# Loads of a unit's r, k, key norms and v placed between the rate products of its preparation (RWKV-7 / sliding-window decoder step)

## The chip, the cores and the metric

The kernel runs on one core of a Trainium2 chip. The core has TensorE (PE; the loading of its weights is shown as PEld), VectorE (DVE), ScalarE (ACT), GpSimd (POOL) and SyncE (SP), which issues nearly all transfers of this kernel (the DMAs). Each engine works through its own instructions in order, and semaphores tie the engines together. The metric is the device time of one execution in microseconds; the median of three runs of the kernel before is 2142.66 us (2141.24 to 2144.08).

## The reference

One inference step of a two-layer trunk for a prompt of 256 tokens, with 16 meta tokens in front, and 8 single-token samples: 280 columns in all. Layer 0 is RWKV-7 time mixing with 64 heads of 64; layer 1 is sliding-window attention with a shared K/V and sinks. The change lies in layer 0. Cut to what matters:

```python
r, k, v, z = (xm[:, :, i] @ w_rkvz[i] for i in range(4))
w_log = -softplus(-(w0 + tanh(xw @ w1) @ w2)) - 0.5
decay = exp(-exp(w_log))
a = sigmoid(a0 + (xa @ a1) @ a2)
kk = k * k_k; kk = kk / max(sqrt(sum(kk * kk, -1)), 1e-12)
k = k * (1 + (a - 1) * k_a); b = kk * a
def rwkv7_step(S, inp):                       # scanned over the tokens
    sa = einsum('bhij,bhj->bhi', S, kk)
    S = S * d - sa[..., None] * b + v[..., None] * k
    return S, einsum('bhij,bhj->bhi', S, r)
y = groupnorm(y) * gn_g + gn_b + sum(r * k * r_k) * v
out = (y * silu(z)) @ w_out
```

Decay and `a` come from two low-rank products, the "rates".

## The kernel before

**Stages.** A first stage normalises the inputs and makes the first k and v products. Then comes phase A, the longest one with several things going on at once; then the output product of layer 0, the shared K/V, layer 1's q and z products with the attention between them, and its output product. All large products run as three fp32r matmuls (high x high, high x low, low x high), whose weights are split into a high and a low part by ScalarE and VectorE (`split`, L183 to L187) as they arrive, five buffers deep.

**Phase A** (`phase_a`, `drive`). `products` lists 64 products of 256 output columns (r, k, v, z, and a first part of the output product), each of 16 *pieces* of six matmuls. `drive` takes one piece after another, and before each it visits generators ("streams"): epilogues of products, `main`, `preps`, `decodes` (the samples), late gates, and side streams such as the group norm. A stream yields a number of pieces to wait, and where needed a condition; it is resumed at the first piece at which both hold. `mark` notes the piece at which something was done, and `after(n, ...)` asks whether it was marked at least n pieces ago. So TensorE's order is written out by hand: what a stream emits on TensorE stands where the piece counter is. The other engines' order is not: the framework's scheduler orders each of them by a simulated timeline in which TensorE's order is fixed, so that a load or a vector operation may stand far ahead of its place in the source, once its inputs and its buffer are free there. One thing holds it back: what a stream other than the first two emits on VectorE is put behind the weight split emitted last but one (`issue_after(self.los[-2].ins)` in `drive`).

**Units.** The 64 heads are 16 units of 4 heads. `preps` prepares unit after unit with `prep(u)`:

- it loads the low-rank weights and visits TensorE four times, 3 to 4 pieces apart, for the rates (`ps_l`, L870 to L872);
- it then waits for the products of r, k, v and, from unit 4 on, for the key norms (`('n', g)`), loads kT, rT and the norms (spread over the rows into kk, L552, two transfers), and forms kk, k, a, the decays' running sum and their exponentials (L887 to L914);
- from unit 4 on it waits for the group norm of the pair two before (`('g', u // 2 - 2)`), since vT of four units ago is then given back after its store to `yd` (L1250), and loads vT (L917);
- it gathers the samples' columns on POOL (L921), turns them on TensorE (`ps_sm`, L924) eight pieces later, and makes two "bonus" products (`ps_bo`, L940), 5 and 4 pieces later. Every visit of TensorE with a `pp_free` condition also waits until a PSUM bank, shared with the epilogues of k and v and the decodes, has had three pieces.

kT has two buffers, rT and kk have one, vT four. `prep_e(u)` forms the matrices KB and E from them (L956 to L968) and is the last reader of rT and kk. For an even unit it runs right behind `prep`; for an odd one `main` runs it (mark `e`), once the pair's chain is done (`u`), the odd unit is prepared (`p`) and the even unit's scores are (`c`). `main` then makes the odd unit's scores (21 pieces), solves the triangular systems (24 + 4 + 7 + 5 = 40), and runs the chain over five chunks of tokens (48); the group norm of the pair ends 46 pieces after its chain (`g`). `preps` begins the next even unit at `e`.

At the end of phase A the gates of the last four blocks are split (`late_gates`, tiles ghi and glo), which the output product `ps_oa` reads first.

Of the kernel before, what the change touches and what calls it, by code (L numbers as in the profile page):

```python
# [109 lines left out]
class Kernel:  # L110
# [736 lines left out]
    def prep(self, u):  # L847
        nc, rp, I = self.nc, self.rp, self.I
        V, A, G = nc.vector, nc.scalar, nc.gpsimd
        tt = V.tensor_tensor  # L850
        MU, AD, SU = ALU.mult, ALU.add, ALU.subtract
        dma = nc.sync.dma_start
        p0 = 2 * u
        b, sl = p0 // 4, slice(p0 % 4, p0 % 4 + 2)
        w = lambda n, bufs=1: rp.tile([128, 2, N], F32, tag=n, bufs=bufs, name=f"{n}{u}")

        raw = rp.tile([LR, 512], F32, tag="lraw", name=f"lraw_{u}")
        dma(raw, I['lw2'][u])
        if u:
            yield 3  # L860
        hi = rp.tile([LR, 512], F32R, tag="lhi", name=f"lhi_{u}")
        lo = rp.tile([LR, 512], F32R, tag="llo", name=f"llo_{u}")
        self.split(hi, lo, raw)
        ws = [(hi[:, 256 * i:256 * i + 256], lo[:, 256 * i:256 * i + 256]) for i in range(2)]
        wa = [w("cl"), w("ta")]
        for i, (hi, lo) in enumerate(ws):
            for j in range(2):
                yield 3 if i or j else 4 if u else 14, self.pp_free
                ps = self.pp_bank(f"ps_l{i}{j}_{u}")
                self.mm3(ps[:, :N], hi[:, j * 128:j * 128 + 128], lo[:, j * 128:j * 128 + 128],  # L870
                         self.lt[i][0], self.lt[i][1], True, True)
                A.activation(wa[i][:, j], ps[:, :N], AF.Tanh, scale=0.5,  # L872
                             bias=self.par2[:, 32 * i + p0 + j:32 * i + p0 + j + 1])
        cl, a = wa
        if u >= 4:
            yield 0, self.after(6, ('n', u // 4), *(('x', m, p0) for m in range(3)))
        else:
            yield 0, self.after(6, ('x', 0, p0))
        kT = w("kT", 2)
        dma(kT, self.kd[b][:, sl])  # L880
        rT = w("rT")
        dma(rT, self.rd[b][:, sl])

        kk = w("kk")
        self.spread(kk, self.kr[u // 4][4 * u % 16:4 * u % 16 + 4])
        for j in range(2):
            V.scalar_tensor_tensor(kk[:, j], kT[:, j], self.pcol(P_KK, p0 + j), kk[:, j], op0=MU, op1=MU)  # L887

        for j in range(2):
            km = rp.tile([128, N], F32, tag="sq", bufs=2, name=f"km{j}_{u}")  # L890
            A.activation(km, a[:, j], AF.Identity, scale=self.par2[:, 64 + p0 + j:65 + p0 + j],
                         bias=self.par2[:, 96 + p0 + j:97 + p0 + j])
            tt(kT[:, j], kT[:, j], km, op=MU)
        A.activation(a, a, AF.Identity, scale=-0.5, bias=self.half[:, 1:2])
        tt(a, a, kk, op=MU)
        A.activation(cl, cl, AF.Identity, scale=0.5, bias=self.half[:, 0:1])

        for j in range(2):
            V.tensor_tensor_scan(cl[:, j, :L], self.reset, cl[:, j, :L], 0.0, op0=MU, op1=AD)

        Pp = self.Pp
        ch = lambda x: x[:, :, :256].rearrange("p q (c t) -> p q c t", t=64)
        pch = Pp[:, :, :260].rearrange("p q (c t) -> p q c t", t=65)
        for j in range(2):
            A.activation(pch[:, j, :, 1:65], ch(cl)[:, j], AF.Exp, scale=-CD)
        A.activation(Pp[:, :, 261:N + 5], cl[:, :, 256:N], AF.Exp, scale=-CD)
        A.activation(cl, cl, AF.Exp, scale=CD)
        if u % 2 == 0:
            self.PC = rp.tile([128, 4, 5], F32, tag="PC", bufs=2, name=f"PC{u}")
        PC = self.PC[:, 2 * (u % 2):2 * (u % 2) + 2]  # L910
        A.copy(PC[:, :, 0:4], pch[:, :, :, 64])
        A.copy(PC[:, :, 4:5], Pp[:, :, 276:277])

        if u >= 4:  # L914
            yield 0, self.after(0, ('g', u // 2 - 2))
        vT = w("vT", 4)
        dma(vT, self.vd[b][:, sl])  # L917

        sm = rp.tile([128, 2, 6, NS], F32, tag="sm", name=f"sm{u}")
        for i, x in enumerate((kk, a, kT, rT, vT, Pp[:, :, 5:])):  # L920
            G.tensor_copy(sm[:, :, i], x[:, :, L:N])  # L921
        yield 8, self.pp_free
        ps = self.pp_bank(f"ps_sm{u}")
        nc.tensor.transpose(ps[:96, :128], sm.rearrange("p a b c -> p (a b c)"), self.ident)  # L924
        sr = rp.tile([96, 2, 64], F32, tag="sr", name=f"sr{u}")
        A.copy(sr, ps[:96, :128].rearrange("p (h j) -> p h j", h=2))
        g, h0 = p0 // 8, (2 * p0) % 16
        for j in range(2):
            dma(self.vecd[g][:, :, h0 + 2 * j:h0 + 2 * j + 2].rearrange("v b h j -> (v b) (h j)"),
                sr[48 * j:48 * j + 48].rearrange("p h j -> p (h j)"))  # L930

        def rk_of(j):
            rk = rp.tile([128, L], F32, tag="sq", bufs=2, name=f"rk{j}_{u}")
            V.scalar_tensor_tensor(rk, rT[:, j, :L], self.pcol(P_RK, p0 + j), kT[:, j, :L], op0=MU, op1=MU)
            return rk
        rk = [rk_of(j) for j in range(2)]
        for j in range(2):
            yield 5 - j if u > 1 else 3, self.pp_free
            ps = self.pp_bank(f"ps_bo{j}_{u}")
            nc.tensor.matmul(ps[:, :L], self.cr[C_BO], rk[j], start=True, stop=True)  # L940
            tt(vT[:, j, :L], ps[:, :L], vT[:, j, :L], op=MU)
            A.activation(vT[:, j, :L], vT[:, j, :L], AF.Identity, bias=self.pcol(P_GB, p0 + j))
        self.U[u] = dict(PC=self.PC, bonus=vT, kT=kT, rT=rT, kk=kk, a=a, cl=cl)
# [998 lines left out]
```

## Time and profile before

| | |
|---|---|
| median of 3 runs | 2142.66 us (2141.24 to 2144.08) |
| profiled execution | 2148.06 us, span 2146.2 us |
| granted TensorE clock over the span | 0.992 |
| weights and other transfers | 446.29 MB, 208 GB/s, DMA engines 66.6% busy on the main queue |
| phase A, 142 to 1306 us | TensorE 1133.8 of 1164.0 us busy, VectorE 905.3, ScalarE 750.6, POOL 98.4 |

The page gives busy times of each engine, the span in slices, the chain of work that ended last, and groups of instructions. Names such as `ps_bo<-rk` are tiles of the program, written and read; `L940` is a line of the kernel. In a list of waits, `PE ps_sm L924 <- POOL sm L921: 2.3, 2, 2.0` means that TensorE stood idle before line 924 until POOL's line 921 was done, 2.3 us in total, twice, 2.0 us at the longest. `SPq` is SP's issuing queue: its time is the issue of a transfer, not the transfer.

### The profile page before, as it was taken

To read this page: it belongs to the slowest core of one execution; us is meant where nothing else is said; L and a number is where in the kernel's file an instruction comes from. 1 tells how busy PE (TensorE), PEld (TensorE's weight loads), DVE (VectorE), ACT (ScalarE), POOL (GpSimd) and SP (SyncE) were. 2 spreads that over 40 slices of the span, in tenths; PEclk is the share of its full clock that TensorE was granted. 3 is DMA by queue.
4 is the path that set the end of the run, shared out by engine and by line. 5 is a ranking of instruction groups with operands and counts; after the bars stand their busy time and mean duration, and the time that the engine had idled before them with its cause. 6 is when DMAs were issued, how large, how long until landed. Compare 5 with 4: busy or idle time off the path is not lost.

```text
span 2146.2 us, 56094 instructions
## 1 busy us (share of the span) xinstructions
PE 2098.6 (98%) x21548; PEld 1993.0 (93%) x21548; DVE 1705.8 (79%) x4080; ACT 1260.3 (59%) x2757; POOL 137.0 (6%) x196
## 2 busy tenths in 40 slices
PE   9999999999999999999999999999999999999997
PEld 7999998899898988898989999999999999999997
DVE  7966767787687777888988787987888888878885
ACT  3456756576765666767666444565565565544443
POOL 0011100011010010100200000100000000000000
PEclk9999999999999999999999999999999999999999
DMA  7998667658756766676656777867445454677774
GB/s 256 311 322 244 194 204 226 205 176 280 221 169 188 240 227 191 212 220 201 208 160 201 232 228 242 239 191 231 146 136 171 145 153 133 172 216 240 224 229 134
DMA packets 275589, 446.29 MB, mean 208 GB/s; under 512 B 53288, under 2 KB 97000, under 8 KB 274928
## 3 DMA queue, kind: packets, MB, share of 16 engines
q1 hardware_dynamic: 274888, 441.66, 66.6%
q8 instruction: 169, 2.77, 0.5%
q10 hardware_dynamic: 432, 1.05, 0.1%
q14 instruction: 100, 0.82, 0.1%
HBM read 381.69 MB, written 65.03 MB: 208 GB/s over the span
## 4 chain that ended last, share of the span: by engine, by line
PE 85%; DVE 5%; DMA 4%; ACT 3%; issue 2%; SPq 0%; POOL 0%; DVEq 0%; POOLq 0%; ACTq 0%
PE ps_z L208 6%; PE ps_z L209 6%; PE ps_z L210 6%; PE ps_r L208 3%; PE ps_ob L208 3%; PE ps_ob L210 3%; PE ps_v L208 3%; PE ps_ob L209 3%; PE ps_q L208 3%; PE ps_q L210 3%; PE ps_q L209 3%; PE ps_k L208 3%; PE ps_r L209 3%; PE ps_r L210 3%; PE ps_v L209 3%; PE ps_v L210 3%
## 5 line engine op out<-in xcount | busy, mean ns | idle before, releaser
L208 PE MATMUL ps_z<-mhlm,whi_z 128*128 128x280 f32 x512 | 158.6, 310 | 0.7 <-ACT st L779 0.7
L208 PE MATMUL ps_q<-bmh,whi_qb 128*128 128x264 f32 x512 | 150.0, 293 | 0.1
L209 PE MATMUL ps_z<-mhlm,whi_z 128*128 128x280 f32 x512 | 149.9, 293 | 0.0
L210 PE MATMUL ps_z<-mhlm,wlo_z 128*128 128x280 f32 x512 | 149.5, 292 | 0.0
L208 PE MATMUL ps_z<-bmh,whi_zb 128*128 128x264 f32 x512 | 147.5, 288 | 0.0
L210 PE MATMUL ps_q<-bmh,wlo_qb 128*128 128x264 f32 x512 | 145.6, 284 | 0.6 <-DVE wlo_qb L187 0.6
L209 PE MATMUL ps_q<-bml,whi_qb 128*128 128x264 f32 x512 | 145.6, 284 | 0.0
L209 PE MATMUL ps_z<-bml,whi_zb 128*128 128x264 f32 x512 | 145.5, 284 | 0.0
L210 PE MATMUL ps_z<-bmh,wlo_zb 128*128 128x264 f32 x512 | 145.4, 284 | 0.0
L208 PE MATMUL ps_ob<-ghi,whi_ob 128*128 128x264 f32 x512 | 145.3, 285 | 0.0
L209 PE MATMUL ps_ob<-glo,whi_ob 128*128 128x264 f32 x512 | 144.6, 283 | 0.0
L210 PE MATMUL ps_ob<-ghi,wlo_ob 128*128 128x264 f32 x512 | 144.6, 284 | 0.0
L185 ACT CAST whi_ob<-raw_ob 128x512 fp32r<-128x512 f32 x128 | 79.1, 620 | 96.7 <-PE ps_ob L209 78.1
L185 ACT CAST whi_oa<-raw_oa 128x512 fp32r<-128x512 f32 x128 | 79.3, 621 | 90.2 <-PE ps_oa L209 32.6
L187 DVE TENSOR_TENSOR wlo_r<-raw_r,whi_r 128x512 fp32r<-128x512 f32 x128 | 87.7, 689 | 50.5 <-ACT whi_r L185 49.5
L208 PE MATMUL ps_v<-mhlm,whi_v 128*128 128x280 f32 x384 | 121.2, 316 | 1.4 <-ACT st L779 1.4
L208 PE MATMUL ps_k<-mhlm,whi_k 128*128 128x280 f32 x384 | 120.0, 312 | 1.3 <-ACT st L779 1.3
L187 DVE TENSOR_TENSOR wlo_v<-raw_v,whi_v 128x512 fp32r<-128x512 f32 x128 | 87.0, 685 | 37.9 <-ACT whi_v L185 35.6
L185 ACT CAST whi_v<-raw_v 128x512 fp32r<-128x512 f32 x128 | 78.9, 618 | 64.9 <-PE ps_v L209 36.1
L185 ACT CAST whi_zb<-raw_zb 128x512 fp32r<-128x512 f32 x128 | 78.2, 619 | 62.6 <-PE ps_z L209 38.1
L209 PE MATMUL ps_k<-mhlm,whi_k 128*128 128x280 f32 x384 | 112.5, 293 | 0.0
L209 PE MATMUL ps_v<-mhlm,whi_v 128*128 128x280 f32 x384 | 112.5, 293 | 0.0
(474 smaller groups left out, 7664.5 us busy)
## 6 DMA issues: line engine op xcount, KB each, us to landing
raw_k<-a_w_rkvz SPq DMA_DIRECT2D x128, 256.0 KB
raw_v<-a_w_rkvz SPq DMA_DIRECT2D x128, 256.0 KB
raw_r<-a_w_rkvz SPq DMA_DIRECT2D x128, 256.0 KB
raw_z<-a_w_rkvz SPq DMA_DIRECT2D x128, 256.0 KB
raw_oa<-a_w_out SPq DMA_DIRECT2D x128, 256.0 KB
raw_qb<-b_w_qz SPq DMA_DIRECT2D x128, 256.0 KB
raw_zb<-b_w_qz SPq DMA_DIRECT2D x128, 256.0 KB
raw_ob<-b_w_o SPq DMA_DIRECT2D x128, 256.0 KB
```

The costliest lines, as they stand in the source:

```text
L185: self.nc.scalar.copy(hi, src)
L187: return self.nc.vector.tensor_tensor(lo, src, hi.bitcast(F32), op=ALU.subtract)
L208: mm(ps, wh, xh, start=start, stop=False)
L209: mm(ps, wh, xl, start=False, stop=False)
L210: return mm(ps, wl, xh, start=False, stop=stop)
```

## The change

In `prep` the conditions for the loads are asked at the visits for the rates, from the second one on. When they hold, rT, kT and kk are loaded there; vT is loaded there too if its own condition holds. The condition for vT asks for six pieces after the group norm, where it asked for none. After the visits: if nothing has been loaded yet, the stream waits for the condition, loads, and in each case yields three pieces before the first use. Later, if vT has not been loaded, it waits for its condition, loads it, and yields four pieces before POOL's copies.

```diff
+        ready = self.after(6, ('n', u // 4), *(('x', m, p0) for m in range(3))) if u >= 4 else \
+            self.after(6, ('x', 0, p0))
+        free = self.after(6, ('g', u // 2 - 2)) if u >= 4 else lambda: True
+        T = {}
+
+        def load(*names):
+            for n in names:
+                T[n] = t = w(n, dict(kT=2, vT=4).get(n, 1))
+                if n == 'kk':
+                    self.spread(t, self.kr[u // 4][4 * u % 16:4 * u % 16 + 4])
+                else:
+                    dma(t, dict(kT=self.kd, rT=self.rd, vT=self.vd)[n][b][:, sl])
         wa = [w("cl"), w("ta")]
         for i, (hi, lo) in enumerate(ws):
             for j in range(2):
...
+                if (i or j) and not T and ready():
+                    load('rT', 'kT', 'kk')
+                if T and 'vT' not in T and free():
+                    load('vT')
         cl, a = wa
-        if u >= 4:
-            yield 0, self.after(6, ('n', u // 4), *(('x', m, p0) for m in range(3)))
-        else:
-            yield 0, self.after(6, ('x', 0, p0))
-        kT = w("kT", 2)
-        dma(kT, self.kd[b][:, sl])
-        rT = w("rT")
-        dma(rT, self.rd[b][:, sl])
-
-        kk = w("kk")
-        self.spread(kk, self.kr[u // 4][4 * u % 16:4 * u % 16 + 4])
+        if not T:
+            yield 0, ready
+            load('rT', 'kT', 'kk')
+            if free():
+                load('vT')
+        yield 3
+        kT, rT, kk = (T[n] for n in ('kT', 'rT', 'kk'))
...
-        if u >= 4:
-            yield 0, self.after(0, ('g', u // 2 - 2))
-        vT = w("vT", 4)
-        dma(vT, self.vd[b][:, sl])
+        if 'vT' not in T:
+            yield 0, free
+            load('vT')
+            yield 4
+        vT = T['vT']
```

## The prediction

> **What bounds the kernel now.** I read the page's busy times first, then its chain, then the stage in which the edited function runs.
>
> ```profile
> span 2146.2 us, 56094 instructions
> PE 2098.6 (98%) x21548; PEld 1993.0 (93%) x21548; DVE 1705.8 (79%) x4080; ACT 1260.3 (59%) x2757; POOL 137.0 (6%) x196
> PE 85%; DVE 5%; DMA 4%; ACT 3%; issue 2%; SPq 0%; POOL 0%; DVEq 0%; POOLq 0%; ACTq 0%
> ```
>
> TensorE is idle for 2146.2 - 2098.6 = 47.6 us in all. An edit that adds or takes away no matmul moves the time through such idle time, and through what follows it on TensorE's clock. Phase A, where `prep` runs, lies between the first `ps_r` and the last `ps_o` product:
>
> ```profile
> L208 PE MATMUL ps_r<-mhld,whi_r x256: 288/292/602, 142.1 to 271.1; 128*128 128x280 f32 x128
> ...
> L208 PE MATMUL ps_o<-mhlm,whi_oa x256: 288/293/438, 1175.7 to 1305.8; 128*128 128x280 f32 x128
> ...
> 142.00:1306.00 1164.00, 1133.82 (x13875) 1062.82 (x13875) 905.27 (x1992) 750.64 (x1634) 98.42 (x143) 0.99 0.69 213
> ```
>
> In that window (the last row's columns are length, then busy time of PE, weight load, DVE, ACT and POOL, clock, DMA) TensorE idles 1164.0 - 1133.8 = 30.2 us. By the code phase A is 64 products of 16 pieces, so a piece lasts 1164 / 1024 = 1.14 us; the last 128 pieces took 130.1 us, 1.02 us each. The waits of TensorE in this stretch, by releaser, largest first (total, times, longest):
>
> ```profile
> PE ps_so L1089 <- DVE TN L1068: 4.8, 2, 2.8
> PE ps_yt L1246 <- DVE vT L1247: 4.0, 1, 4.0
> PE ps_wu L1188 <- ACT W L1180: 2.8, 2, 2.2
> PE ps_so L1095 <- issue: 2.3, 4, 1.4
> PE ps_sm L924 <- POOL sm L921: 2.3, 2, 2.0
> ...
> PE ps_sc L1000 <- DVE RB L1009: 1.1, 1, 1.1
> ```
>
> No row is a transfer of `prep`. The question is which of these the edit can take away, and which it can add.
>
> **The loads.** The edit issues the same transfers: per unit one kT, one rT, two halves of kk, one vT. Bytes: no change. Are they late today? In the queue of SP and on VectorE around unit 5 (start, length; then duration and first and last start):
>
> ```profile
> 415.36 0.61 SPq L552 DMA_DIRECT2D kk<-kr  x1
> 416.07 0.82 SPq L882 DMA_DIRECT2D rT<-rd  x1
> ...
> L967 DVE TENSOR_TENSOR E<-rT,Pp x1: 180/180/180, 415.3 to 415.3; 128x32 f32<-128x32 f32 x1
> ...
> L887 DVE SCALAR_TENSOR_TENSOR kk<-kT,par,kk x2: 495/496/496, 442.1 to 442.5; 128x280 f32<-128x280 f32 x2
> ```
>
> rT and kk have one buffer each. Unit 4's last reader of rT ends at 415.3 + 0.18 = 415.5; kk's transfer goes at 415.4 and rT's at 416.1, 26 us ahead of the first use at 442.1. So the order in the queues isn't the order of the source: loads already go as soon as their buffer is free. Writing them ahead cannot free the buffer sooner. Over the stretch after 300 us VectorE waited for a kk load once:
>
> ```profile
> DVE kk L887 <- DMA kk<-kr: 3.5, 1, 3.5
> ```
>
> vT is held by its buffer too: its load sits at the head of SP's queue until the store that empties the buffer lands.
>
> ```profile
> SPq L917 <- DMA yd<-vT: 23.0, 10, 4.6
> ```
>
> That wait holds up the weight loads queued behind it on SP. If vT goes as soon as now, it stays; if the later condition (6 pieces after `g`) really delays the issue, up to 23.0 us of SP's waiting goes, which is not TensorE's: the weights are buffered five deep. I cost all moved loads at 0, the kk row apart. What hides them is the 26 us of lead; without that cover each unit would show a wait like kk's 3.5.
>
> **The one late load.** It is unit 4's, whose key norms have only just been written. VectorE is in order, and stood still for it; then TensorE stood for VectorE:
>
> ```profile
> 375.14 0.18 DVE L1062 TENSOR_TENSOR stmp<-NL 128x28 f32<-128x28 f32 x1
> 378.83 0.93 DVE L887 SCALAR_TENSOR_TENSOR kk<-kT,par,kk 128x280 f32<-128x280 f32 x2 [3.51 <-DMA kk<-kr]
> ...
> 384.54 0.45 DVE L1247 SCALAR_TENSOR_TENSOR vT<-ps_yt,par,vT 128x272 f32<-128x272 f32 x1
> ...
> 385.05 0.55 PE L1246 MATMUL ps_yt<-consts,Y 128*128 128x128 f32 x3 [4.02 <-DVE vT L1247]
> ...
> 385.00:386.00 1.00, 0.95 (x6) 0.95 (x7) 1.00 (x2) 1.00 (x2) 0.00 (x0) 0.79 0.00 0
> 386.00:389.00 3.00, 3.00 (x14) 3.00 (x14) 1.67 (x5) 3.00 (x6) 0.00 (x0) 0.50 0.75 236
> ```
>
> Queued behind kk were the scans, a weight split and the substitution; the old vT's product came last. The price is 4.0 us of idle TensorE and, with the clock at 0.79 and 0.50, another 0.21 x 1 + 0.50 x 3 = 1.7: 5.7 us. The added `yield 3` in place of `yield 0` (which costs one piece) puts this block two pieces later, and VectorE's work of this stream is tied behind a recent weight split, so kk moves about 2 x 1.14 = 2.3 us down VectorE's order: a wait of 1.2 stays of 3.5, and of TensorE's 4.0 some 1.7. The ends are 0 (VectorE still waits) and -5.7 (the rest of the substitution runs first and all cover it). I take -2.3 and half the clock's 1.7: **-3**.
>
> **The first unit's transpose.** `ps_sm` waited 2.0 us at 171.3 for POOL's copies:
>
> ```profile
> L924 PE MATMUL ps_sm<-consts,sm x16: 270/272/415, 171.3 to 1113.6; 128*96 128x128 f32 x16
> ```
>
> It moves two pieces later, but the copies' sources do as well: between -2.0 and 0; I take **-1**.
>
> **Places in TensorE's order.** This is what the edit really moves. I count a pair of units from the moment its odd predecessor's matrices are formed (`e`). Main: scores 21, solve 40, chain 48, so `e` again after 109 + 1. Group norm of the chain just ended: `g` at 45. Before: the even unit waits for `g` at 45, then 1 + 8 + 5 + 4, done at 63; the odd one needs 16 for the rates, 1, 1, 17: done at 98, 12 pieces ahead of main. After: the even unit waits to 45 + 6, then 4 + 8 + 5 + 4, done at 72 to 73; the odd one finds its v free and needs 16 + 3 + 17 = 36: done at 108 to 109. The slack falls from 12 pieces to 1. Besides, visits wait for a PSUM bank: unit 5's two bonus products are 4 pieces apart by the code, and stood here (first start of the window; then the second):
>
> ```profile
> L940 PE MATMUL ps_bo<-rk,crbo x8: 392/392/497, 469.2 to 537.6; 128*128 128x272 f32 x8
> ...
> 481.05 0.62 PE L940 MATMUL ps_bo<-rk,crbo 128*128 128x272 f32 x2
> ```
>
> About 12 us, 7 pieces over 4.5 us. Unit 11's stand as far apart, by the chain of waits:
>
> ```profile
> 867.01 0.66 PE ps_bo L940 x2
> 879.73 0.72 PE ps_bo L940 x2
> ```
>
> Where that falls the next pair begins up to 7 pieces late, so the last chain ends some 14 pieces late at most, 14 x 1.02 = 14 us. The cover is at the end:
>
> ```profile
> L209 PE MATMUL ps_oa<-glo,whi_oa x62: 287/291/297, 1306.3 to 1330.0; 128*128 128x280 f32 x62
> L187 DVE TENSOR_TENSOR glo<-gy,ghi x4: 1309/1311/1317, 1282.2 to 1293.2; 128x1120 fp32r<-128x1120 f32 x4
> ```
>
> The last gate is split by 1293.2 + 1.3 = 1294.5. It feeds the fourth group of 8 of those matmuls, 0.39 us apart (23.7 / 61), so from 1306.3 + 24 x 0.39 = 1315.6: 21 us of cover. Cost 0; without cover, 14.
>
> **New waits.** The odd unit's bonus products, the even unit's copies to KB and E and the next pair's begin now crowd into the last pieces of a pair, on a VectorE busy 905.3 of 1164.0 us (78%). No row shows it; the nearest are `ps_sc` waiting for VectorE, 1.1 once, and `ps_so`, 4.8 / 2 = 2.4 each. Six pairs follow unit 4. Ends: -4 (the solve's VectorE work loses the rk and bonus work that ran beside it, so the `ps_so` rows, 4.8 and 2.3, shrink by about half) and 6 x 2.4 = +14. Nearer to the first row: one wait of 1.1 in most pairs, **+5**.
>
> Sum: -3 - 1 + 5 = +1 us on the profiled execution's 2148.06 us (span 2146.2), which lies 5.4 over the median 2142.66: 2149 there, **2143.7** for the median. I call it no change.
>
> What a wait costs beside itself: around a 2.1 us wait at the end of phase A the clock was
>
> ```profile
> 1290.00:1300.00 10.00, 7.89 (x49) 7.67 (x48) 7.86 (x12) 4.68 (x7) 0.00 (x0) 0.83 0.97 312
> ```
>
> 0.17 x 10 = 1.7 us lost on top. The Trainium skill (TensorE: Matmul & The Clock Gate, What's actually happening) says that the clock halves after an idle window of about 3.4 us. By that rule waits of 1 to 2.4 us would cost themselves alone and the slower rival below would end near 2146.9; the row goes against it.
>
> **Rivals.**
>
> *Faster: the late kk is all that mattered.* The unit-4 wait goes whole with its clock (-5.7), `ps_sm` too (-2.0), and the crowding adds nothing: 2142.66 - 7.7 = 2135. For it: both have their rows, and the move is the right way. Against: they sit at two units of 16, and other waits get new places. The Trainium skill (DMA: Bandwidth & Descriptors, Rules for kernel authors) advises to issue a transfer early and wait late, which speaks for this rival; the trace shows that issue is already early in 15 units.
>
> *Slower: preparation ends where main begins.* With one piece of slack, in three of six pairs the scores or the solve find VectorE busy, each with a `ps_so`-like wait and its clock: 3 x (2.4 + 1.7) = 12.3; less 3 of the kk: 2142.66 + 9.3 = 2152. It decides from the second such wait on. For it: the count above. Against: main's work is put first on VectorE.
>
> *Slower still: the end runs out of cover.* If bank waits push every one of six pairs by 7 pieces, 42 x 1.02 = 43 us against 21: +22, 2165. Against: only two units show such waits.
>
> *It does what it says.* If loads really go earlier, what they can bring is the one kk row, with its clock: 2142.66 - 5.7 = 2137. For it: `ready` is asked up to 9 pieces sooner. Against: the buffers held as shown, and unit 4's norms, which aren't written sooner. Its chance is a part of the faster rival's.
>
> **How the numbers follow.** Waits re-dealt near balance 0.42, faster rival 0.24, slower rival 0.28, end rival 0.06. About 0.2% (4.3 us) is what a measurement of this kernel can tell from no change. The first case spans 2137 to 2150: 0.09 of its chance lies below 2138.4, 0.22 within, 0.11 above. Faster: 0.09 + 0.24 + 0.02 of the slower rival's edge = 0.35. Same: 0.22. Slower: 0.11 + 0.26 + 0.06 = 0.43. The range takes in the faster rival with 3 us to spare and the slower one with 6: 2132 to 2158; the likeliest case's own is 2137 to 2150.
>
> **What would show it.** Kk and rT still issued within 1 us of the last read of E; kk's wait at unit 4 shorter and `ps_yt`'s 4.0 us at 385 down or gone, with the clock whole at 386 to 389; unit pairs with sm some 10 pieces later after `g` in even units; last glo between 1295 and 1309 with no wait at the first `ps_oa`. Wrong, if loads lead their use by clearly more than now, or if idle time of phase A moves from 30 us by more than 8 in either direction.

## The result, and the profile after

The changed kernel takes 2153.91 us (median; 2150.35 to 2158.61), the kernel before beside it 2143.57: the ratio is 1.0047 [1.0033, 1.0061], **10.3 us slower**. That lies inside the range, 10 us above the predicted 2143.7, which stood for no change, and outside the 2137 to 2150 of the likeliest case: it is the range's width, made for the slower rival, that holds it. One profiled execution of it took 2152.39 us against 2148.06 before, 4.3 us more, so the profile holds only part of the loss; a single execution of this kernel can lie 5 us from its median, and what follows is read for its kind more than for its size.

The page's span, busy times and chain, and the window of phase A (length; busy time of PE, weight load, DVE, ACT, POOL; clock, DMA share, GB/s) of the changed kernel:

```profile
span 2150.6 us, 56110 instructions
PE 2101.7 (98%) x21548; PEld 1996.5 (93%) x21548; DVE 1710.9 (80%) x4080; ACT 1260.2 (59%) x2757; POOL 137.8 (6%) x196
PE 89%; DVE 4%; ACT 3%; issue 2%; DMA 2%; SPq 0%; DVEq 0%; POOLq 0%; ACTq 0%
142.00:1309.00 1167.00, 1135.26 (x13852) 1064.68 (x13851) 904.73 (x1983) 748.58 (x1631) 99.21 (x143) 0.98 0.68 211
```

The matmuls are as many as before, and TensorE's idle time in phase A is 1167.0 - 1135.3 = 31.7 us, against 30.2. The idle total hardly moved; yet the span grew by 4.4 us, and PE is "busy" 3.1 us longer with the same matmuls, over a lower clock: 0.98 in the window against 0.99. So the question is not how much TensorE waits but which waits it has. TensorE's waits in this stretch, largest first (total, times, longest):

```profile
PE ps_v L209 <- issue: 4.8, 1, 4.8
PE ps_dy L1321 <- DVE dy L1318: 3.3, 1, 3.3
PE ps_r L208 <- issue: 3.2, 1, 3.2
PE ps_v L208 <- ACT st L779: 2.9, 1, 2.9
PE ps_so L1108 <- issue: 2.3, 3, 1.1
PE ps_sy L1204 <- ACT X L1203: 2.3, 1, 2.3
```

The rows at the head of the old list have gone or shrunk: `ps_yt` waiting 4.0 for VectorE's vT and `ps_sm` 2.3 for POOL are no longer there, and `ps_so` waits 0.6 for TN where it waited 4.8. In their place stand other single waits of 2 to 5 us, two of them "issue" (the engine waited for nothing that the profile shows). What one such wait costs beside itself; the first row is the 2.3 us wait at `ps_sy`, the second the time behind it:

```profile
1127.90:1130.20 2.30, 0.01 (x2) 0.00 (x1) 2.28 (x4) 2.18 (x7) 0.20 (x1) 0.99 0.50 117
1130.20:1140.40 10.20, 10.20 (x67) 9.47 (x68) 5.79 (x15) 4.00 (x11) 0.61 (x2) 0.50 0.39 117
```

After 2.3 us of idling the clock stands at half for 10.2 us. TensorE is counted as busy all that time; at half clock that is an estimated 5.1 us of work.

What happened to the loads, in SP's queue and on VectorE around unit 5:

```profile
421.09 0.62 SPq L552 DMA_DIRECT2D kk<-kr  x1
421.81 0.53 SPq L876 DMA_DIRECT2D rT<-rd  x1
...
L980 DVE TENSOR_TENSOR E<-rT,Pp x1: 184/184/184, 421.0 to 421.0; 128x32 f32<-128x32 f32 x1
...
L899 DVE SCALAR_TENSOR_TENSOR kk<-kT,par,kk x2: 502/504/505, 452.8 to 453.2; 128x280 f32<-128x280 f32 x2
```

They still go within 1 us of the read of E that frees their buffer (421.0), now 31 us ahead of the use at 452.8 in place of 26: the use moved, not the load.

### The profile page after: what moved, and what is told of

It is laid out like the page before. It is cut to its first block, busy times and chain, and to the rows that moved or that the text cites. A ratio compares the mean times of both kernels' runs of the same rounds, so it can differ in the third digit from the quotient of the medians.

```text
span 2150.6 us, 56110 instructions
## 1 busy us (share of the span) xinstructions
PE 2101.7 (98%) x21548; PEld 1996.5 (93%) x21548; DVE 1710.9 (80%) x4080; ACT 1260.2 (59%) x2757; POOL 137.8 (6%) x196
## 4 chain that ended last, share of the span: by engine, by line
PE 89%; DVE 4%; ACT 3%; issue 2%; DMA 2%; SPq 0%; DVEq 0%; POOLq 0%; ACTq 0%
PE ps_z L208 6%; PE ps_z L209 6%; PE ps_z L210 6%; PE ps_k L208 3%; PE ps_v L208 3%; PE ps_ob L208 3%; PE ps_ob L210 3%; PE ps_ob L209 3%; PE ps_q L208 3%; PE ps_q L210 3%; PE ps_q L209 3%; PE ps_r L208 3%; PE ps_v L209 3%; PE ps_k L209 3%; PE ps_v L210 3%; PE ps_k L210 3%
## 5 line engine op out<-in xcount | busy, mean ns | idle before, releaser
L208 PE MATMUL ps_z<-mhlm,whi_z 128*128 128x280 f32 x512 | 161.5, 315 | 1.2 <-ACT st L779 1.2
L209 PE MATMUL ps_z<-mhlm,whi_z 128*128 128x280 f32 x512 | 151.6, 296 | 0.0
L208 PE MATMUL ps_k<-mhlm,whi_k 128*128 128x280 f32 x384 | 118.9, 310 | 0.0
L210 PE MATMUL ps_v<-mhlm,wlo_v 128*128 128x280 f32 x384 | 113.3, 295 | 0.0
```

The costliest lines, as they stand in the source:

```text
L208: mm(ps, wh, xh, start=start, stop=False)
L209: mm(ps, wh, xl, start=False, stop=False)
L210: return mm(ps, wl, xh, start=False, stop=stop)
```

## The experiments

Twelve kernels ran, each beside the kernel before on the same chip. They ask three things: is it the loads or the places; is it the places of `main` or of the preparations; and does the stream of instructions itself play a part. The profiles are of one execution each.

**The loads alone.** The loads at the changed places of the source, TensorE's visits where they were:

```diff
-        yield 3
+        else:
+            yield 0
...
-            yield 0, free
+            yield 0, self.after(0, ('g', u // 2 - 2))
             load('vT')
-            yield 4
+        elif u >= 4:
+            yield 0
```

> Loads written at the rate visits as in the change, but every visit of TensorE at its old piece (no added three pieces, none of the ten before the turn of an even unit). Theory (the loads are held by their buffers, so what moved is the places): within 0.2% of before, 2139 to 2148 us, with unit 4's wait for kk of 3.5 us and ps_yt's 4.0 us still there. Rival (the earlier loads crowd SP's queue and the transfers): about 2150 to 2154, as the changed kernel.

Measured: 2146.44 us against 2146.01, ratio 0.9998 [0.9986, 1.0009]: no change. In the traces ScalarE, GpSimd and SyncE run the order of the kernel before; on TensorE two neighbouring small matmuls, on VectorE four single instructions of 4080, one kk among them, have changed places. The source order of the loads was not their queue order, so there was nothing to move. Both waits at unit 4 are still there in its list:

```profile
DVE kk L900 <- DMA kk<-kr: 3.6, 1, 3.6
...
PE ps_yt L1261 <- DVE vT L1262: 4.1, 1, 4.1
```

**The places alone.** The changed pieces, each load in the source right before its first use:

```diff
-                if (i or j) and not T and ready():
-                    load('rT', 'kT', 'kk')
+                if (i or j) and not R and ready():
+                    R.add('r')
...
         yield 3
+        load('kT', 'rT', 'kk')
...
-        if 'vT' not in T:
+        if 'v' not in R:
             yield 0, free
-            load('vT')
             yield 4
+        load('vT')
```

> The counterpart: the visits stand at the changed kernel's pieces, while every load is written right before its first use. Theory: as the changed kernel, 2150 to 2158 us. Rival (loads): within 0.2% of before.

Measured: 2154.61 us, ratio 1.0040 [1.0025, 1.0054]: the whole loss of the change. In the traces it has the changed kernel's instruction order but for a load of kk and one of v's weights that change places in SP's queue, one weight split on VectorE and two pairs of small matmuls, and its list of waits is headed by the same rows:

```profile
PE ps_v L209 <- issue: 4.8, 1, 4.8
PE ps_dy L1321 <- DVE dy L1318: 3.3, 1, 3.3
```

So the pieces that the edit adds (`yield 3`, `yield 4`, six after the group norm) are what costs; the loads are not.

**Each half of the places.** The yield of three alone (v as before), and the v part alone (six pieces after `g`, four more before POOL's copies):

```diff
 e3:
-            yield 0, free
+            yield 0, self.after(0, ('g', u // 2 - 2))
...
-            yield 4
+        elif u >= 4:
+            yield 0
 e4:
-        yield 3
+        else:
+            yield 0
```

> The change without its second half: the added three pieces before the first use of r, k and kk, while v's condition and the turn of the even unit stand as before. If the crowding at the end of a pair (ten pieces on the even unit) is what costs, this one stays within 0.2% of before, about 2139 to 2147; if any shift of the places deals the waits anew, it lands anywhere from 2138 to 2156.

> The other half alone: v's condition six pieces later and four pieces after its load, everything before that at its old piece. Crowding: most of the change's ten us, 2149 to 2155. Waits dealt anew: anywhere from 2138 to 2156, and not the sum of the parts.

Measured: 2161.38 us, 1.0066 [1.0051, 1.0082], and 2176.32 us, 1.0139 [1.0122, 1.0156]: +15 and +30 us, and together +10. Both lie above all that was expected of them (2156 at most). The parts don't add, so neither has a price of its own. In the second the chain ends later still: the late gates' split (VectorE), and the clock and idling of the window ahead of the first `ps_oa` (1334.5 us):

```profile
L187 DVE TENSOR_TENSOR glo<-gy,ghi x4: 1316/1320/1325, 1332.1 to 1346.1; 128x1120 fp32r<-128x1120 f32 x4
...
1306.00:1334.00 28.00, 26.16 (x215) 25.60 (x214) 19.78 (x61) 10.03 (x18) 0.00 (x0) 0.94 0.78 247
```

The first one has no such tail. Counted in pieces of its products, in four of the six pairs from unit 4 on it keeps 10 to 17 pieces between an odd unit's preparation and main (12 to 20 before), and still loses 15 us: a lack of slack isn't what costs it. In the other two, those of units 5 and 11, one piece is left, and so it was in the kernel before.

**The preparations alone, without the loads' edit.** The kernel before with one, and with two more pieces before its rate visits of every unit but the first:

```diff
-            yield 3
+            yield 4
```

> The kernel before with every unit's preparation but the first begun one piece later (4 pieces for 3 after its low-rank weights are loaded), and nothing else. If any move of these places deals TensorE's waits anew and before is a favourable deal, it is slower by 3 to 15 us, though the slack of 12 pieces is hardly touched; if the change's own crowding is the cause, it stays within 0.2%.

(the second with `yield 5`)

> The kernel before with every preparation but the first begun two pieces later, where it was one: main stays within a piece of its old place. Theory M: within 0.2% of before, as with one piece. Rival P: slower by 5 to 15 us, as the three added pieces (two net) were.

Measured: 2145.61 us, 1.0007 [0.9994, 1.0019], and 2152.52 us, 1.0027 [1.0015, 1.0038]. Main stands within a piece of its old place in the first and within two in the second. One piece costs nothing, where 3 to 15 us were expected if any move costs; two cost about 6 us, where nothing was expected if only main's place counts. So neither simple rule holds.

**Main alone.** The kernel before with main held back once, by three and by eight pieces, after the matrices of unit 5 (the third pair):

```diff
+                if o == 1:
+                    yield 3
```

> The kernel before, in which only main pauses: three pieces once, ahead of the odd scores of the third pair. From there on main, its group norms and the preparations stand two to three pieces later against the weight products, as in the kernel with the three added pieces alone, but no preparation is longer. Theory M (what costs is where solve and chain fall against the product boundaries): slower by 5 to 15 us, 2151 to 2161. Rival P (what costs is preparation's own place against main): within 0.2% of before.

(the second with `yield 8`)

> The same with eight pieces, the slip of the changed kernel up to its eleventh unit. Theory M: again slower, 2149 to 2161, by an amount that needn't be larger than with three. Rival P: within 0.2%.

Measured: 2155.24 us, 1.0039 [1.0026, 1.0052], and 2157.76 us, 1.0055 [1.0042, 1.0069]. Nothing of a unit's preparation became longer, no load was moved in the source, and the loss is about that of the change, as expected of main's place: +9.3 and +11.8 us. The phase A window and the largest waits of the first:

```profile
142.00:1316.00 1174.00, 1141.36 (x13873) 1069.55 (x13872) 906.22 (x1991) 747.87 (x1633) 95.66 (x143) 0.98 0.69 211
...
PE ps_so L1097 <- issue: 4.6, 4, 2.2
PE ps_so L1091 <- DVE TN L1070: 4.0, 2, 2.3
PE ps_yt L1248 <- DVE vT L1249: 3.7, 1, 3.7
PE ps_z L210 <- issue: 2.9, 1, 2.9
```

Idle 1174.0 - 1141.4 = 32.6 us, 2.4 more than before; clock 0.98. The same signature as after: about as much idling, in other places, more of it "issue", and a lower clock.

**The one late load alone.** The kernel before with three pieces for unit 4 only:

```diff
+        if u == 4:
+            yield 3
```

> The kernel before with the three added pieces at unit 4 alone, the one unit whose key norms came late. Main stands where it stood. The prediction's step for that wait: VectorE's wait of 3.5 us for kk falls to about 1, ps_yt's 4.0 us with it, 2 to 5 us faster, 2140 to 2144. Rival: VectorE reaches kk as early as before and nothing changes, 2145 to 2147.

Measured: 2143.1 us against 2145.94, ratio 0.9984 [0.9974, 0.9995]: 2.8 us faster, as expected, and the fastest version of the study; its profiled execution (2138.71) is one of the fastest of its twelve. By pieces, TensorE's order is that of the kernel before. VectorE's kk no longer waits, TensorE's `ps_yt` doesn't either, and the clock of the stretch is whole:

```profile
378.12 0.93 DVE L889 SCALAR_TENSOR_TENSOR kk<-kT,par,kk 128x280 f32<-128x280 f32 x2
...
381.33 0.55 PE L1248 MATMUL ps_yt<-consts,Y 128*128 128x128 f32 x3
...
378.00:390.00 12.00, 11.40 (x325) 10.73 (x324) 11.09 (x23) 6.45 (x17) 3.41 (x5) 1.00 0.60 175
...
142.00:1297.00 1155.00, 1126.87 (x13875) 1056.26 (x13874) 904.85 (x1992) 749.82 (x1633) 98.37 (x143) 1.00 0.70 214
```

**The stream of instructions.** "Issue" waits of phase A grew from 2.8 us to 10.3. The largest, in TensorE's timeline of the changed kernel (start, length, and in brackets the idle time before):

```profile
790.46 1.23 PE L1108 MATMUL ps_so<-TR,ET 32*16 32x16 f32 x127 [1.15 <-issue]
791.62 0.40 PE L208 MATMUL ps_v<-mhlm,whi_v 128*128 128x280 f32 x1
796.79 0.60 PE L209 MATMUL ps_v<-mhlm,whi_v 128*128 128x280 f32 x1 [4.77 <-issue]
...
791.60:796.80 5.20, 0.43 (x12) 0.20 (x2) 1.54 (x3) 0.36 (x1) 0.20 (x1) 0.56 1.04 401
796.80:802.50 5.70, 5.70 (x25) 5.44 (x27) 0.69 (x1) 1.15 (x3) 0.00 (x0) 0.50 0.34 113
```

It comes after 127 small matmuls of the solve within 1.2 us, with the DMA engines full (1.04), and in the middle of a product: nothing that one engine hands to another. Such a burst uses up many instructions in little time, and instructions are fetched too: the page of the changed kernel, like that of the one before, has

```profile
q8 instruction: 169, 2.77, 0.5%
```

169 packets of 16.4 KB, for 21548 matmuls and as many weight loads: 255 for each packet. The Trainium skill (Runtime: NRT & Kernel Launch, Instruction fetch mechanics) says that an engine's instructions come in blocks of 16 KiB, 256 of them, fetched while the block before runs, the crossing being mostly hidden. The packets agree with the size; that the crossing is hidden holds for most of them, but not at this burst. The traces keep the time of every packet. Between 789 and 794 us none ran; between 794.0 and 795.3:

```profile
q8 instruction: 1, 0.02, 4.9%
```

It ran from 794.2 to 795.2, 2.2 us after TensorE had stopped, and TensorE went on 1.6 us behind its end. So it is everywhere: each of the 65 issue waits over 0.2 us that the 14 profiles hold between the first `ps_r` and the first `ps_oa` ends 1.2 to 1.6 us after such a packet, of which there is one in 10.7 us; of the 310 other waits 9 do. The issue waits are waits for instructions. To test it by displacement, the 7 filling matmuls in the first stage, whose result nobody reads, were replaced by many short ones, so that everything behind stands further down the stream. The trace has two records for each of these matmuls, and a weight load for each record: the displacement is 114 or 50 matmuls with as many weight loads, 228 or 100 instructions, where the expectation below counted half of that:

```diff
-            filling(7)
+            for _ in range(64):
+                nc.tensor.matmul(junk[:, :16], ones, fill[:, :16], start=True, stop=True)
```

> The changed kernel with its seven filling matmuls before the first k product replaced by 64 short ones, so that everything TensorE does later stands 114 rows (64 - 7 matmuls and as many weight loads) further along its instruction stream; the places in phase A and the loads are the same. Theory A (a third of the loss is TensorE waiting for blocks of its own instructions, 256 rows each, which the bursts of small solve matmuls use up in 1.2 us): the waits that the profile ends with issue, 10.1 us in the changed kernel, move and shrink to about 3 to 6, and the time falls 4 to 8 us, to 2146 to 2150. Theory B (those waits come with the places): still 9 to 11 us of them, and 2153 to 2156.

(the kernel before with the same edit)

> The same displacement in the kernel before, whose issue waits are 2.6 us. Theory A: they grow, to 4 to 10 us, and the time by 2 to 8 us, 2148 to 2154. Theory B: still 2 to 4 us, and within 0.2% of before, 3 us of start included.

(the changed kernel with 32)

> The changed kernel displaced by 50 rows of TensorE's stream (32 short matmuls for the seven). Theory A: another amount of issue waits than at 0 and at 114 rows. Theory B: 9 to 11 us of them again, 2153 to 2156.

Measured: 2175.47 us, 1.0150 [1.0130, 1.0171]; 2172.87 us, 1.0128 [1.0113, 1.0144]; 2158.53 us, 1.0060 [1.0044, 1.0077]. The edit had a cost of its own that swamps the rest. The same stretch of the first stage in the changed kernel, and below it with the 64 short fillings:

```profile
15.30:39.20 23.90, 23.15 (x99) 18.51 (x99) 23.06 (x55) 7.88 (x13) 0.00 (x0) 1.00 0.54 188
```

```profile
15.30:39.20 23.90, 23.90 (x105) 22.99 (x105) 22.89 (x53) 7.87 (x13) 0.00 (x0) 0.50 0.27 102
```

The short matmuls don't hold the clock up, and the first product of phase A starts at 162.8 us instead of 141.7. So the three totals say nothing on the fetch, whatever was expected of them. What can be read is the issue waits of phase A: 10.3 us after, 11.2 with 64, 5.1 with 32; 2.8 before, 5.1 with 64. They move with the displacement. The first was expected to fall to 3 to 6; but its 228 instructions are nearly a whole packet of 255, after which the packets' bounds fall almost where they fell, and that may be why it didn't. The other two came as expected of the fetch (4 to 10 in the second, another amount than 10.3 in the third). The distance of the two kernels, both with 64, is 2175.47 - 2172.87 = 2.6 us in place of 10.3, 1.2 of it from the start of phase A (162.8 against 161.6). That speaks for the fetch as a part of the loss, with a disturbed start in both.

**The profiles side by side.** For each kernel: the length from the first `ps_r` to the first `ps_kv` product (the end of the work around phase A), the sum of TensorE's waits over 0.2 us from the first `ps_r` to the first `ps_oa`, the issue waits among them, and the time in that stretch for which the clock's records stand at one half. That time comes in pieces of 3.41 us in every kernel, so it is given as their count. The sum is (waits, less those of before) + half of (time that TensorE is busy at half clock, less that of before); it should give the length's growth. Of the sum, "fetch" is what the issue waits and the halved stretches begun behind them make up: a stretch is counted there if most of TensorE's idling in the 5 us ahead of it is issue waits, so this column is an estimate.

| kernel | median ratio | length, us | waits, us | issue, us | halves | sum, us | of it fetch, us | length's growth, us |
|---|---|---|---|---|---|---|---|---|
| before | 1 | 1263.4 | 29.8 | 2.8 | 6 | | | |
| unit 4 alone | 0.9984 | 1254.4 | 27.7 | 3.2 | 2 | -8.9 | -1.2 | -8.9 |
| loads alone | 0.9998 | 1263.5 | 28.0 | 3.5 | 7 | 0.0 | -1.0 | +0.2 |
| preparations +1 | 1.0007 | 1262.2 | 29.9 | 3.9 | 4 | -3.2 | -0.5 | -1.1 |
| preparations +2 | 1.0027 | 1270.6 | 33.0 | 6.0 | 9 | +6.5 | +5.0 | +7.3 |
| main +3 | 1.0039 | 1273.7 | 32.0 | 7.4 | 11 | +9.7 | +9.5 | +10.4 |
| main +8 | 1.0055 | 1274.4 | 37.4 | 11.3 | 9 | +10.9 | +10.5 | +11.0 |
| places alone | 1.0040 | 1268.9 | 32.6 | 9.4 | 9 | +5.5 | +8.9 | +5.5 |
| after | 1.0047 | 1269.3 | 31.2 | 10.3 | 11 | +7.6 | +10.3 | +5.9 |
| three alone | 1.0066 | 1272.5 | 36.6 | 8.8 | 8 | +10.1 | +9.4 | +9.2 |
| v alone | 1.0139 | 1295.6 | 47.6 | 8.4 | 13 | +29.3 | +8.7 | +32.2 |

Waits and halved clock together give the growth within 3 us in every row. The kernels that are no slower have 2 to 7 halves and under 4 us of issue waits; the slower ones 8 to 13 and 6 us or more. In six of the seven slower kernels the fetch column makes up most of the sum or all of it; only "v alone" loses more elsewhere. In the changed kernel the waits grow by 1.4 us and the halves by five. Of the eleven, 4.7 us are idle time that is in the waits already, so the halves add 6.2 us.

## Why the prediction was right or wrong

**The loads: right.** Costed at 0 because they go when their buffer comes free; e1 measures 0.9998, e2 the full loss without them, and the rows at 421 show the same 1 us.

**The late load of unit 4: right in size, but not kept.** The wait of VectorE was to shrink from 3.5 to 1.2 us; it measures 1.5, and `ps_yt` waits no more. In the changed kernel TensorE is held up a moment later by a bank's copy instead, and the clock halves all the same:

```profile
377.09 0.51 DVE L899 SCALAR_TENSOR_TENSOR kk<-kT,par,kk 128x280 f32<-128x280 f32 x1 [1.52 <-DMA kk<-kr]
...
384.83 0.40 PE L208 MATMUL ps_v<-mhlm,whi_v 128*128 128x280 f32 x1 [2.89 <-ACT st L779]
...
386.00:389.40 3.40, 3.40 (x17) 3.32 (x16) 1.12 (x3) 0.92 (x3) 0.00 (x0) 0.51 1.01 339
```

There 2.9 + 0.49 x 3.4 = 4.6 us are lost, of 5.7 before: a gain of 1.1 where 3 was forecast, and the sign "clock whole at 386 to 389" fails. Done by itself the same move brings 2.8 us, the forecast's 3. The prediction had named the rest of the substitution as what could cover the wait, but not a product's own bank as the next to come late.

**The first unit's transpose: about right.** Its 2.0 us wait is gone from the list, the better end of its two; 1 was taken.

**The places: right in kind, short in size.** Counted in pieces of the products, main falls 8 pieces behind its old place by unit 5 and 20 by the last pair, where at most 14 was forecast. It goes in steps: 4 by the first pair, 4 more at unit 5 and 12 more at unit 11. The slack was misjudged there: the prediction counted 12 pieces before and 1 after for every pair, but at units 5 and 11 preparation ended one piece before main already in the kernel before, so that each added piece pushed main on; in the other four pairs 12 to 20 pieces became 13, 2, 22 and 5. The 7 pieces of bank waits, from which the 14 was made, aren't what came: after the change the two bonus products of units 5 and 11 stand 4 pieces apart, as written. The end shows it: the last split of the gates is done 21.6 us later than before (1316.1 against 1294.5), past the 1309 that the prediction had as its limit, and as forecast it still makes no wait at the first `ps_oa`:

```profile
L187 DVE TENSOR_TENSOR glo<-gy,ghi x4: 1316/1322/1326, 1301.4 to 1314.8; 128x1120 fp32r<-128x1120 f32 x4
```

The rival of the end, given 0.06, is only touched: with the v half alone the gates are split from 1332.1 on and `ps_oa` begins at 1334.5, but the idling and clock of the window ahead of it are 1.8 + 0.06 x 28 = 3.5 us, and two waits just behind its begin 2.4 us, of that kernel's 30.

**The new waits: the step that failed.** The prediction put it as "one wait of 1.1 in most pairs, **+5**", from crowding at a pair's end. With -1.1 and -2.0 for the two steps above, the median's +10.3 leaves about +13 for it, near its upper end of +14, and the single profiled execution's +4.3 about +7. The mechanism was wrong as well as the size. Crowding isn't needed: main alone, three pieces later once with nothing crowded, costs 9.3 us, and the kernel that keeps 10 pieces of slack or more in four pairs costs 15. What the runs show in its place is that the waits are dealt again, with about the same total, and that waits for instructions come up among them. The prediction's sum has no term for these: it took the row `ps_so` "issue", 2.3 us, for VectorE work of the solve. In the changed kernel the waits for other engines fall from 27.0 to 20.9 us, `ps_so` for TN from 4.8 to 0.6 as the favourable end had it, but the issue waits rise from 2.8 to 10.3, with two of 4.8 and 3.2 us that no row of before stood for. With the halved clock behind them these make an estimated +10.3 us in the profiled execution, and all else -2.7. A long wait is often followed by 3.4 us or more at half clock, but not always (in "unit 4 alone" two of the four waits over 2 us are not). Waits over 2 us are six before and six after; the halved stretches are six and seven, of which two now last three pieces.

**The rivals.** The measured time is next to the slower rival's 2152 (0.28), but that is luck: its mechanism, a preparation ending where main begins, was there at units 5 and 11 before the change too. The faster rival, 2135, had the right rows: `ps_yt`'s wait for vT and `ps_sm`'s are gone. It failed because other waits came, and unit 4's move alone brings 2.8 us of its 5.7. "It does what it says" fell with e1.

**Left open.** Why the packets come late in one order and not in another: they run all along phase A, some 110 of them, and only 3 to 6 make a wait in a kernel whose start is undisturbed. A displacement of the stream that leaves the clock alone at the start would show it, and wasn't tried. Open is also what makes up the 20 us that "v alone" loses beside it, and how much of the median's 10.3 us is fetching, since the profiled execution lost 4.3.

## What to carry to other kernels

Before loads are written earlier, look whether their issue already follows the release of their buffer; if it does, the only thing that moves is the rest of the code. Where one unit of many has a late load, give that unit alone the extra room: here it brought 2.8 us, and three pieces in every unit cost 15. In an order tuned by hand, a move is priced by the waits that it deals again and the halved clock behind each, and the quickest test of that is to make the move with nothing else. A wait that ends with "issue" is to be held against the times of the instruction packets before it is put down to an engine.

## What the hardware showed that was not expected

- The clock halves after waits shorter than the Trainium skill (TensorE: Matmul & The Clock Gate, What's actually happening) has it. It gives one idle window of about 3.4 us; here 2.3 us of idling were followed by 10.2 us at 0.50 (1130.2 to 1140.4), a stretch with small products of the chain, which may have kept it there. The time at half clock came in pieces of 3.41 us in every profile, which agrees with its window.
- Short matmuls did not keep the clock up: with 64 matmuls of 16 columns in place of 7 of 280, TensorE counted as busy 23.90 of 23.90 us and the clock stood at 0.50 throughout; with 32 it was 0.73 over the same stretch.
- TensorE stood still for 4.8 us in the middle of a product, after 127 small matmuls in 1.2 us and with the DMA engines at 1.04, because its instructions weren't there: the packet of 16.4 KB began 2.2 us after it had stopped, and it went on 1.6 us after the packet's end. Every issue wait over 0.2 us of phase A, 65 in 14 profiles, ends 1.2 to 1.6 us behind such a packet.
